# One hybrid encoder layer on one core: row factors put into the raw operands of the input projection

## The chip, the core and the metric

The kernel runs on one core of a Trainium2 chip. The core has a matrix engine (TensorE, PE in the profile, with PEld for its weight loads), a vector engine (VectorE, DVE), a scalar engine (ScalarE, ACT), a general engine (GpSimd, POOL), a queue engine (SyncE, SP) that issues most of the transfers, and transfer engines (DMA). Each engine works off its own queue in order; semaphores tie the queues together. Operands lie in on-chip memory, matmul sums in PSUM. The metric is the device time of one execution in microseconds, lower is better.

## The reference

One layer of a streaming encoder: token mixing, cross-attention into 256 memory tokens, and a SwiGLU feed-forward part, each between two RMS norms, for 2048 tokens of 1024 numbers in float32. What matters here is the start:

```python
def rms_norm(x, g):
    xf = x.astype(jnp.float32)
    y = xf * lax.rsqrt(jnp.mean(xf * xf, axis=-1, keepdims=True) + RMS_EPS)
    return (y * g.astype(jnp.float32)).astype(x.dtype)
...
        u = rms_norm(h, g_mix_pre[l])
        z = u @ w_in[l]
        qa, ka, va, qh, fh, ih, gh = jnp.split(z, IN_SPLITS, axis=-1)
...
    qf = jax.nn.silu(q.astype(f32)) * (Dk ** -0.5)
...
    f = lbf + (1.0 - lbf) * jax.nn.sigmoid(f_logit.astype(f32))
...
    o = rms_norm(o, onorm_g) * jax.nn.silu(g.astype(f32))
```

The columns of z are split into queries, keys and values of a windowed attention (qa, ka, va) and four groups for a gated recurrence (qh through a silu, fh through a sigmoid, ih as it is, gh through a silu). A row's norm is a factor r of that token; the weight g belongs to the column of x.

## The kernel before

Every matrix product is done with float32 operands that are split into a rounded high part and a remainder (the low part); three matmuls (high x high, high x low, low x high) stand for one. For large products the kernel also saves matmuls by a seven-product scheme: two 2x2 block matrices are multiplied with seven block products in place of eight, at the cost of sums and differences of the operands and of the results.

The change concerns the first stage, `in_first` (from L440), which computes z for the first 1024 of the 2048 tokens, transposed (columns of w_in on the partitions). It goes through eleven blocks (`ORDER`, L427), each of two times 128 columns of z: block 0 is columns 4 and 5 (in units of 128), block 1 is 0 and 1, block 2 is 2 and 3, blocks 3 to 6 pair a column of fh (10 to 13) with one of qh (6 to 9), blocks 7 and 8 are ih (14 to 17), blocks 9 and 10 are gh (18 to 21). A block has a kind: "p", plain, with eight products in four steps (`eight`, L1132), or "o", with seven products in seven steps (`seven`, L1092, in the order 1, 5, 6, 3, 7, 2, 4). A product is 12 matmuls of 128x512. So a plain block is 96 matmuls and a seven-product block 84. Before the change, blocks 0 and 1 are plain.

The moving operand is x transposed, in four raw tiles `raw[q, s]` (q: half of the 1024 columns of x, s: half of the tokens). `first` (L457) multiplies a raw tile by the weight g and splits it, ACT for the high part, DVE for the low one; the four pairs are the operands named 1, 2, 8 and 3 of the products (tiles named u in the profile). `gained` (L466) puts g into the raw tiles themselves, with ACT. From these, `resident` (L959) makes the operands of the seven products that are sums or differences (5, 7, 6, 4 in this order; DVE at L981, in place), each in two halves of 128x1024, split by `split2` (L949: ACT at L952, DVE at L955; tiles named T). 1, 2 and 3 are taken over from `first`. `phases` (L1169) writes out the order: after each step it makes the weight operands of the step after next, advances the generators that stand beside the blocks (twice a step in a plain block), finishes one half of an operand (`split`) and starts another (`half`). Operands that are a raw block by themselves (1, 2, 3, 8) are finished two steps after they are started, and, by `behind` (L1015), behind whatever each engine already has; sums and differences have no such lag. Seven slots hold operands: four that hold the operands of `first` until their last use, and three more, of which two hold the staged rows of x at the start.

The weight operands of a block come through `streamed` (L1030): two raw tiles are loaded, seven operands are formed by DVE sums (L1057), split by ACT or POOL for the high part and by DVE (L955) for the low part; tiles named S.

The norm is applied to the products, not to x. `rows` loads the 1024 rows of x (L477), `squares` (L480) sums their squares on ACT, POOL makes r of it (L108 and L111 in `rstd`), `spread` (L490) turns r into a 128x512 tile by transposes on PE, and `known` (L498) has ACT copy it into `r_bc` (L501), beside block 2. Blocks whose outputs come before that (0 and 1) copy them out bare (L590) and are multiplied by r_bc on POOL later (L620). In the others `out` (L582) multiplies each 128x512 output: by DVE straight from PSUM where there is nothing to add (L593, one a block), else DVE adds a stored part (L595) and POOL multiplies (L596, three a block). Then fh goes through ACT's tanh (L598) and POOL (L600); qh and gh through tanh (L604) and DVE (L605). A block of fh and qh then runs the decays of the recurrence (`decays`, L688) in the time of the block behind it: logarithm on ACT (L693), two scans on DVE (L697), POOL subtracts (L702), exponentials on ACT (L711, L713), products on DVE (L716, L628).

The order on each engine is not quite the written one: a scheduler that is fed with the written order moves an instruction ahead where it expects its engine to be free.

Of the kernel before, what the change touches and what calls it, by code (L numbers as in the profile page):

```python
# [11 lines left out]
F32 = mybir.dt.float32  # L12
F32R = mybir.dt.float32r
I32 = mybir.dt.int32
AF = mybir.ActivationFunctionType
# [33 lines left out]
class Layer:  # L49
# [390 lines left out]
    def in_first(self):  # L440
# [6 lines left out]
        key = {(0, 0): 1, (1, 0): 2, (0, 1): 8, (1, 1): 3}  # L447
        self.r_bc = None

# [15 lines left out]

        def gained(q, s):  # L466
            for k in range(4):
                nc.scalar.activation(raw[q, s][:, k, :], raw[q, s][:, k, :], AF.Copy,
                                     scale=g_t[:, 4 * q + k:4 * q + k + 1])

        def rows():

            for s in range(2):
                stage.append(self.tb.tile([P, 4, D], F32, tag="T", name=f"x0_{s}", bufs=3))
            for s in range(2):
                for i in range(4):
                    self.load(stage[s][:, i, :], I["x"][(4 * s + i) * P:(4 * s + i + 1) * P, :])  # L477
# [20 lines left out]
        def known():  # L498
            r = self.gain_tile()
            for s in range(2):  # L500
                nc.scalar.activation(r[:, s * 512:(s + 1) * 512], spread(0, s), AF.Copy)  # L501
            self.r_bc = r
            yield

# [24 lines left out]
        def parted():  # L529
            for n in (1, 3, 2, 0):  # L530
# [5 lines left out]
                with self.behind() if n else contextlib.nullcontext():  # L536
# [29 lines left out]
    def in_block(self, ca, cb, beside, get, between):  # L566
# [15 lines left out]
        def out(i, j, a, b):  # L582
            if not z:
                z.append(self.pair_tile())
                bare.append(self.r_bc is None)
            c0 = (ca, cb)[i] * P
            sl = slice(j * 512, (j + 1) * 512)
            zs = z[0][:, i, sl]
            if bare[0]:
                nc.scalar.activation(zs, a, AF.Copy)  # L590
                return
            if b is None:
                nc.vector.tensor_tensor(zs, a, self.r_bc[:, sl], ALU.mult)  # L593
            else:
                nc.vector.tensor_tensor(zs, a, b, ALU.add)  # L595
                nc.gpsimd.tensor_tensor(zs, zs, self.r_bc[:, sl], ALU.mult)  # L596
# [572 lines left out]
    def phases(self, jobs, first, prologue=None):  # L1169
# [18 lines left out]
        for g, (n, i, p) in enumerate(steps):  # L1188
            key = (n, p, i > len(jobs[n][2]) // 2 if p == 8 else 0)
# [64 lines left out]
        class Ready(dict):  # L1254


            def __getitem__(_, p):
                q = next(q for q in range(g, len(steps)) if steps[q][2] == p)
                n, i, _ = steps[q]
                key = (n, p, i > len(jobs[n][2]) // 2 if p == 8 else 0)  # L1260
                while left.get(key, 1):
# [489 lines left out]
```

## Time and profile before

| what | value |
|---|---|
| time, median of 3 runs (lowest to highest) | 2576.51 us (2575.25 to 2578.38) |
| the profiled execution: its time; its span | 2576.22 us; 2574.5 us |
| mean granted TensorE clock | 0.994 |
| matmuls | 12000 |
| busy PE, DVE, ACT, POOL | 2515.8, 1766.2, 1258.9, 518.3 us |
| read from and written to HBM | 330.45 MB, 162.53 MB |

The stage of the change takes the first 256 us of the span; what follows it is not touched. In rows of the profile, `out<-in` are the program's tiles, x is a count, and after the bar stand the busy time of the group in us, the mean duration of one in ns, and the idle time of the engine ahead of them with what ended it. In a timeline, a row is the start and the duration in us, the engine, the line and the operation, and in brackets the engine's idle time before it. In a table of stretches, PEclk is the granted TensorE clock as a share of full speed.

### The profile page before, as it was taken

To read this page: it belongs to the slowest core of one execution; us is meant where nothing else is said; L and a number is where in the kernel's file an instruction comes from. 1 tells how busy PE (TensorE), PEld (TensorE's weight loads), DVE (VectorE), ACT (ScalarE), POOL (GpSimd) and SP (SyncE) were. 2 spreads that over 40 slices of the span, in tenths; PEclk is the share of its full clock that TensorE was granted. 3 is DMA by queue.
4 is the path that set the end of the run, shared out by engine and by line. 5 is a ranking of instruction groups with operands and counts; after the bars stand their busy time and mean duration, and the time that the engine had idled before them with its cause. 6 is when DMAs were issued, how large, how long until landed. Compare 5 with 4: busy or idle time off the path is not lost. (4 is left out here: it accounts for less than half of the span.)

```text
span 2574.5 us, 34140 instructions
## 1 busy us (share of the span) xinstructions
PE 2515.8 (98%) x12000; PEld 2093.7 (81%) x12000; DVE 1766.2 (69%) x2790; ACT 1258.9 (49%) x2632; POOL 518.3 (20%) x666
## 2 busy tenths in 40 slices
PE   8989999999999999999999999999999999999998
PEld 6767788878897888888788888888888888888886
DVE  7777678877766678697775665575666566664756
ACT  7452366655655575565564333353333344543443
POOL 2663343321321334224310000000000000000022
PEclk9999999999999999999999999999999999999999
DMA  5452655484896787767983552253555434566798
GB/s 198 138 203 95 199 151 173 132 258 160 262 315 236 229 279 212 244 230 209 313 264 126 167 165 81 82 196 123 181 195 197 159 129 140 194 217 191 222 223 206
DMA packets 277835, 495.22 MB, mean 192 GB/s; under 512 B 20896, under 2 KB 135584, under 8 KB 277152
## 3 DMA queue, kind: packets, MB, share of 16 engines
q1 hardware_dynamic: 264128, 443.76, 51.5%
q0 software_dynamic: 11232, 40.90, 8.4%
q10 hardware_dynamic: 2304, 8.39, 0.8%
q8 instruction: 94, 1.54, 0.2%
q14 instruction: 77, 0.63, 0.1%
HBM read 330.45 MB, written 162.53 MB: 191 GB/s over the span
## 5 line engine op out<-in xcount | busy, mean ns | idle before, releaser
L1088 PE MATMUL psm<-T,S 128*128 128x512 f32 x2664 | 1032.7, 391 | 8.6 <-ACT S L952 4.4
L1089 PE MATMUL psm<-T,S 128*128 128x512 f32 x2664 | 1039.3, 390 | 0.0
L1090 PE MATMUL psm<-T,S 128*128 128x512 f32 x2664 | 1033.1, 390 | 1.5 <-DVE S L955 1.5
L1088 PEld LDWEIGHTS psm<-T,S 128*128 128x128 f32 x2664 | 501.0, 188 | 116.0 <-ACT S L952 5.2
L1090 PEld LDWEIGHTS psm<-T,S 128*128 128x128 f32 x2664 | 500.8, 188 | 107.3 <-DVE S L955 3.1
L1089 PEld LDWEIGHTS psm<-T,S 128*128 128x128 f32 x2664 | 501.2, 188 | 102.9
L952 ACT ACTIVATE S<-sum 128x512 fp32r<-128x512 f32 (+1 forms) x338 | 207.2, 617 | 331.7 <-PE psm L1090 328.9
L955 DVE TENSOR_TENSOR S<-sraw,S 128x512 fp32r<-128x512 f32 (+1 forms) x311 | 217.1, 704 | 212.8 <-ACT S L952 203.2
L955 DVE TENSOR_TENSOR S<-sum,S 128x512 fp32r<-128x512 f32 (+1 forms) x404 | 283.7, 707 | 81.8 <-ACT S L952 67.3
L1103 ACT ACTIVATE part<-psm 128x512 f32<-128x512 f32 x297 | 174.7, 591 | 204.1 <-PE psm L1090 197.0
L952 ACT ACTIVATE S<-sraw 128x512 fp32r<-128x512 f32 (+1 forms) x272 | 166.4, 617 | 154.8 <-PE psm L1090 149.5
L1458 POOL DMA_DIRECT2D row<-y_d x28 | 25.1, 895 | 1071.2 <-DMA sraw<-hid_d 905.3
L1429 ACT ACTIVATE junk<-row 128x512 f32<-128x512 f32 x160 | 99.6, 624 | 95.2 <-DVE row L1451 32.8
L172 PE MATMUL psg<-u,wlo 128*128 128x512 f32 x352 | 141.6, 402 | 2.4 <-DVE wlo L153 2.4
L955 DVE TENSOR_TENSOR T<-row,T 128x1024 fp32r<-128x1024 f32 x104 | 124.1, 1202 | 27.7 <-ACT T L952 27.3
L170 PE MATMUL psg<-u,whi 128*128 128x512 f32 x352 | 142.7, 406 | 0.0
L171 PE MATMUL psg<-u,whi 128*128 128x512 f32 x352 | 141.8, 403 | 0.0
L952 ACT ACTIVATE T<-row 128x1024 fp32r<-128x1024 f32 x104 | 105.3, 1023 | 20.5 <-DMA row<-in_w_down_dram 9.9
L1633 DVE TENSOR_TENSOR part<-psm,part 128x512 f32<-128x512 f32 x66 | 45.5, 689 | 65.7 <-PE psm L1090 65.6
L954 POOL TENSOR_SCALAR S<-sum 128x512 fp32r<-128x512 f32 x66 | 50.3, 763 | 183.5 <-PE psm L1090 105.5
L1090 PE MATMUL psm<-u,S 128*128 128x512 f32 x172 | 71.4, 418 | 13.1 <-DVE S L955 13.1
L1624 DVE TENSOR_TENSOR row<-psm,part 128x512 f32<-128x512 f32 x66 | 45.5, 689 | 54.7 <-PE psm L1090 54.6
(326 smaller groups left out, 3664.2 us busy)
## 6 DMA issues: line engine op xcount, KB each, us to landing
sraw<-in_w_gate_dram SPq DMA_DIRECT2D x44, 512.0 KB, 4.8
sraw<-in_w_up_dram SPq DMA_DIRECT2D x44, 512.0 KB, 5.0
hid_d<-row SPq DMA_DIRECT2D x44, 512.0 KB, 2.7
h_d<-row SPq DMA_DIRECT2D x32, 512.0 KB, 6.6
y_d<-row SPq DMA_DIRECT2D x32, 512.0 KB, 3.6
sraw<-hid_d SPq DMA_DIRECT2D x32, 512.0 KB, 5.0
row<-h_d POOLq DMA_DIRECT2D x30, 512.0 KB, 7.1
row<-y_d POOLq DMA_DIRECT2D x28, 512.0 KB, 7.6
```

The costliest lines, as they stand in the source:

```text
L170: nc.tensor.matmul(ps, ah, bh, start=(i == 0), stop=False)
L171: nc.tensor.matmul(ps, ah, bl, start=False, stop=False)
L172: nc.tensor.matmul(ps, al, bh, start=False, stop=(i == n - 1))
L952: self.nc.scalar.activation(hi, raw, AF.Copy)
L954: self.nc.gpsimd.tensor_scalar(hi, raw, 1.0, 1.0, ALU.mult, ALU.mult)
L955: self.nc.vector.tensor_tensor(lo, raw, f32(hi), ALU.subtract)
L1088: nc.tensor.matmul(ps, s[:, 0, k, :], t[:, 0, k, :], start=st, stop=False, **kw)
L1089: nc.tensor.matmul(ps, s[:, 0, k, :], t[:, 1, k, :], start=False, stop=False, **kw)
L1090: nc.tensor.matmul(ps, s[:, 1, k, :], t[:, 0, k, :], start=False, stop=sp, **kw)
L1103: nc.scalar.activation(t, ps, AF.Copy)
L1429: self.nc.scalar.activation(junk, a, AF.Square, scale=float(D) ** -0.5, accum_out=to)
L1624: nc.vector.tensor_tensor(d, a, c, ALU.add)
```

## The change

Three blocks are plain instead of two. They work on operands from x times g, without r, as blocks 0 and 1 did. Once r is known for half of the tokens, DVE multiplies the raw tiles in place by g and r (r read from PSUM). All seven operands of the seven-product blocks (3 to 10) are then made from these normed raw tiles, so their outputs need no factor. `gained` is gone; the first four tiles of rows of x are loaded right behind the transposed x, and the other four within block 0; the squares move from block 1 to block 0 and `known` from block 2 to block 1. The seven products become a second job of `phases`, and no operand of it is started until `held` is cleared at the end of `known`. Operand 3 is put ahead of 7, since 7 is formed in place on the raw tile of 3. Outputs of blocks 1 and 2 are multiplied by r on DVE from PSUM; block 0's are multiplied on POOL later, as before. In blocks 3 to 10 an output of ih that has nothing to be added to is copied by ACT, and the tanh and the product behind it read PSUM where nothing is added.

```diff
+        self.r_bc = self.r_half = None
+        self.held = True
...
-        def gained(q, s):
-            for k in range(4):
-                nc.scalar.activation(raw[q, s][:, k, :], raw[q, s][:, k, :], AF.Copy,
-                                     scale=g_t[:, 4 * q + k:4 * q + k + 1])
...
+        def rows(s):
+            stage.append(self.tb.tile([P, 4, D], F32, tag="T", name=f"x0_{s}", bufs=3))
+            for i in range(4):
+                self.load(stage[s][:, i, :], I["x"][(4 * s + i) * P:(4 * s + i + 1) * P, :])
 
         def squares():
 
+            rows(1)
             for s in range(2):
...
         def known():
             r = self.gain_tile()
             for s in range(2):
-                nc.scalar.activation(r[:, s * 512:(s + 1) * 512], spread(0, s), AF.Copy)
-            self.r_bc = r
-            yield
+                ps = spread(0, s)
+                nc.scalar.activation(r[:, s * 512:(s + 1) * 512], ps, AF.Copy)
+                self.r_bc = r if s else self.r_bc
+                self.r_half = r
+                for q in ((0, 1), (1, 0))[s]:
+                    for k in range(4):
+                        t = raw[q, s][:, k, :]
+                        nc.vector.scalar_tensor_tensor(t, t, g_t[:, 4 * q + k:4 * q + k + 1], ps, ALU.mult, ALU.mult)
+                    yield
+                if s == 0:
+                    yield
+            self.held = False
...
-        beside = [(), (), (0, 1), (2, 3), (4, 5), (6,), (7,), (), (), (), ()]
+        beside = [(), (), (), (0, 1), (2, 3), (4, 5), (6, 7), (), (), (), ()]
         get = fetch()
-        blocks = [("p" if i < 2 else "o",)
+        blocks = [("p" if i < 3 else "o",)
...
-        job = (lambda i, j, a, n: raw[i, j][:, a:a + n, :], 4, blocks, None,
-               {0: [rows], 1: [squares], 2: [known], 8: [scaled], 10: [parted]})
-        phases = self.phases([job], T)
+        jobs = [(of, 4, blocks[:3], None, {0: [squares], 1: [known]}),
+                (of, 4, blocks[3:], None, {5: [scaled], 7: [parted]})]
+        phases = self.phases(jobs, T)
...
+        rows(0)
         first(0, 0)
...
-        for q, s in ((1, 1), (0, 1), (0, 0), (1, 0)):
-            gained(q, s)
         self.mix_consts()
...
             if b is None:
-                nc.vector.tensor_tensor(zs, a, self.r_bc[:, sl], ALU.mult)
+                if ca < 6:
+                    nc.vector.tensor_tensor(zs, a, self.r_half[:, sl], ALU.mult)
+                    return
             else:
                 nc.vector.tensor_tensor(zs, a, b, ALU.add)
-                nc.gpsimd.tensor_tensor(zs, zs, self.r_bc[:, sl], ALU.mult)
-            if C_FH <= c0 < C_IH:
-                nc.scalar.activation(zs, zs, AF.Tanh, scale=0.5)
+                a = zs
+            if C_IH <= c0 < C_GH:
+                if b is None:
+                    nc.scalar.activation(zs, a, AF.Copy)
+            elif C_FH <= c0 < C_IH:
+                nc.scalar.activation(zs, a, AF.Tanh, scale=0.5)
                 h = (c0 - C_FH) // P
                 nc.gpsimd.tensor_scalar(zs, zs, self.fb[:, h:h + 1], self.fa[:, h:h + 1], ALU.mult, ALU.add)
-            elif C_QH <= c0 and not C_IH <= c0 < C_GH:
+            else:
...
-                nc.scalar.activation(t, zs, AF.Tanh, scale=0.5)
-                nc.vector.scalar_tensor_tensor(zs, t, 1.0, zs, ALU.add, ALU.mult)
+                nc.scalar.activation(t, a, AF.Tanh, scale=0.5)
+                nc.vector.scalar_tensor_tensor(zs, t, 1.0, a, ALU.add, ALU.mult)
...
-        queue = sorted(uses, key=lambda k: (uses[k][0] - (5 if k[1] == 7 and jobs[k[0]][3] is None else 0), k))
+        queue = sorted(uses, key=lambda k: (uses[k][0] - (5 if k[1] == 7 and jobs[k[0]][3] is None else
+                                                          6 if k[1] == 3 and first else 0), k))
...
-                if not queue:
+                if not queue or first and self.held:
                     return False
```

More of the change, by code (lines that the diff above doesn't have):

```diff
@@ L464, in first @@
                                                ALU.mult, ALU.subtract)
-        def gained(q, s):
-            for k in range(4):
-                nc.scalar.activation(raw[q, s][:, k, :], raw[q, s][:, k, :], AF.Copy,
-                                     scale=g_t[:, 4 * q + k:4 * q + k + 1])
[L471 to L477, printed above, removed]
-            yield
+        def rows(s):
+            stage.append(self.tb.tile([P, 4, D], F32, tag="T", name=f"x0_{s}", bufs=3))
+            for i in range(4):
+                self.load(stage[s][:, i, :], I["x"][(4 * s + i) * P:(4 * s + i + 1) * P, :])
         def squares():
+            rows(1)
             for s in range(2):
@@ L539, in parted, with of @@
                 u[s] += [(t[:, 0, k, :], t[:, 1, k, :]) for k in range(4)]
[L541 removed]
+        beside = [(), (), (), (0, 1), (2, 3), (4, 5), (6, 7), (), (), (), ()]
         get = fetch()
[L543 removed]
+        blocks = [("p" if i < 3 else "o",)
                   + self.in_block(*p, beside[i], get if i > 6 else (), None if i else lambda: x_load(0, 0))
                   for i, p in enumerate(self.ORDER)]
[L546 to L548 removed]
+        def of(i, j, a, n):
+            return raw[i, j][:, a:a + n, :]
+        jobs = [(of, 4, blocks[:3], None, {0: [squares], 1: [known]}),
+                (of, 4, blocks[3:], None, {5: [scaled], 7: [parted]})]
+        phases = self.phases(jobs, T)
         self.load(g_t, I["g_mix_t"])
@@ L1188, in phases @@
         for g, (n, i, p) in enumerate(steps):
-            key = (n, p, i > len(jobs[n][2]) // 2 if p == 8 else 0)
+            key = (n, p, i > len(jobs[n][2]) // 2 if p == 8 and not first else 0)
             uses.setdefault(key, []).append(g)
-        queue = sorted(uses, key=lambda k: (uses[k][0] - (5 if k[1] == 7 and jobs[k[0]][3] is None else 0), k))
+        queue = sorted(uses, key=lambda k: (uses[k][0] - (5 if k[1] == 7 and jobs[k[0]][3] is None else
+                                                          6 if k[1] == 3 and first else 0), k))
         slots = [("A", -2, i) for i in range(4)] + [("B", -1, i) for i in range(3)]
@@ L1259, in __getitem__ @@
                 n, i, _ = steps[q]
-                key = (n, p, i > len(jobs[n][2]) // 2 if p == 8 else 0)
+                key = (n, p, i > len(jobs[n][2]) // 2 if p == 8 and not first else 0)
                 while left.get(key, 1):
```

4 lines of the change are left out of this document (1 added, 3 removed).

## The prediction, made before the changed kernel was run

> **What bounds the kernel now.** I read the page first, then the busy times of each engine by stretch, then the waits of TensorE and the timelines around one wait.
>
> ```profile
> span 2574.5 us, 34140 instructions
> ...
> PE 2515.8 (98%) x12000; PEld 2093.7 (81%) x12000; DVE 1766.2 (69%) x2790; ACT 1258.9 (49%) x2632; POOL 518.3 (20%) x666
> ```
>
> TensorE is busy for 98% of the span, so only two things can move the end: the number of matmuls, and the few places where PE stands still or runs slowly. The change touches the first 256 us alone. There the stretches, cut at the blocks of the first half (block 2, 3, 4, 5, 6, 7, then 8 and 9, then 10), read:
>
> ```profile
> core 0: us, PE busy (x) PEld busy (x) DVE busy (x) ACT busy (x) POOL busy (x), PEclk, DMA share, GB/s
> 56.00:78.00 22.00, 22.00 (x101) 18.03 (x100) 11.91 (x13) 6.10 (x11) 15.90 (x10) 1.00 0.39 145
> 78.00:101.00 23.00, 23.00 (x101) 18.49 (x99) 18.73 (x22) 9.15 (x14) 12.76 (x12) 1.00 0.43 136
> 101.00:127.00 26.00, 21.79 (x85) 16.61 (x84) 19.91 (x21) 14.29 (x22) 16.48 (x17) 0.93 0.29 102
> 127.00:152.00 25.00, 20.87 (x83) 16.51 (x83) 18.84 (x22) 14.63 (x23) 15.43 (x17) 0.93 0.58 210
> 152.00:177.00 25.00, 21.81 (x87) 16.89 (x86) 20.03 (x24) 14.32 (x22) 16.02 (x18) 0.93 0.59 206
> 177.00:204.00 27.00, 24.51 (x102) 19.48 (x101) 20.28 (x28) 9.98 (x18) 13.29 (x15) 0.94 0.33 121
> 204.00:241.00 37.00, 36.98 (x163) 29.68 (x161) 30.81 (x41) 8.91 (x15) 13.91 (x13) 1.00 0.20 71
> 241.00:256.00 15.00, 14.12 (x59) 10.97 (x60) 9.01 (x13) 5.64 (x9) 7.68 (x6) 1.00 0.44 154
> ```
>
> Blocks 2 and 3 lose nothing. Blocks 4 to 7 lose 4.2 + 4.1 + 3.2 + 2.5 = 14.0 us of PE idle time, and their granted clock is 0.93 to 0.94: 0.07 of 26, 25 and 25 us and 0.06 of 27 us make another 6.9 us. In all 20.9 us can be won there, and hardly anything elsewhere. What the waits are, and how one of them comes about:
>
> ```profile
> L1090 PE MATMUL psm<-u,S 128*128 128x512 f32 x40 | 18.8, 471 | 13.1 <-DVE S L955 13.1
> ```
>
> ```profile
> 98.92 0.39 PE L1088 MATMUL psm<-T,S 128*128 128x512 f32 x1
> ...
> 100.79 0.40 PE L1090 MATMUL psm<-T,S 128*128 128x512 f32 x1
> ...
> 105.82 0.79 PE L1090 MATMUL psm<-u,S 128*128 128x512 f32 x1 [3.88 <-DVE S L955]
> 106.41 0.63 PE L1088 MATMUL psm<-u,S 128*128 128x512 f32 x1
> 106.84 0.63 PE L1089 MATMUL psm<-u,S 128*128 128x512 f32 x1
> ```
>
> ```profile
> 93.17 3.00 POOL L596 TENSOR_TENSOR pair<-pair,g 128x512 f32<-128x512 f32 x2 [0.63 <-DVE pair L595]
> ...
> 103.32 1.90 POOL L702 TENSOR_TENSOR pair<-pair,d_mid 128x1024 f32<-128x1024 f32 x1
> ```
>
> ```profile
> 93.61 3.11 DVE L955 TENSOR_TENSOR S<-sum,S 128x512 fp32r<-128x512 f32 x2
> ...
> 100.61 2.33 DVE L697 TENSOR_TENSOR_SCAN pair<-reset,pair 128x512 f32<-128x512 f32 x2
> 102.86 0.67 DVE L593 TENSOR_TENSOR pair<-psm,g 128x512 f32<-128x512 f32 x1
> 103.44 2.33 DVE L955 TENSOR_TENSOR S<-sraw,S 128x512 fp32r<-128x512 f32 x1
> ```
>
> The first two rows are eight matmuls apart, so matmuls start 0.234 us apart. At 105.82 one has waited 3.88 us for the low part of the block's first weight operand, a DVE subtraction (L955). That subtraction stood behind two scans of the decays and a multiplication by the row factors (L593), and then took 2.33 us because POOL's L702 ran beside it. The scans came late because POOL multiplied two outputs by the factors first (L596, 3.00 us) before ACT's tanh and POOL's L600 could go on. After the wait the next matmuls are 0.43 us apart for 1.5 us or so. All four waits (13.1 us) have this form. So the bound in blocks 4 to 7 is DVE's queue, stretched and fed late by POOL.
>
> **The change part by part.** Prices come from these rows of the first 260 us:
>
> ```profile
> L468 ACT ACTIVATE pair<-pair,g_t 128x512 f32<-128x512 f32 x16 | 11.2, 709 | 0.0
> ```
>
> ```profile
> L596 POOL TENSOR_TENSOR pair<-pair,g 128x512 f32<-128x512 f32 x27 | 42.3, 1574 | 25.3 <-DVE pair L595 25.0
> L620 POOL TENSOR_TENSOR pair<-pair,g 128x1024 f32<-128x1024 f32 x4 | 9.9, 2512 | 4.1 <-ACT g L501 4.1
> ```
>
> ```profile
> L955 DVE TENSOR_TENSOR S<-sum,S 128x512 fp32r<-128x512 f32 x36 | 34.9, 985 | 6.1 <-ACT S L952 3.4 <-POOL S L954 2.6
> L595 DVE TENSOR_TENSOR pair<-psm,part 128x512 f32<-128x512 f32 x27 | 18.3, 687 | 19.8 <-PE psm L1090 19.5 <-ACT part L1103 0.2
> L525 DVE SCALAR_TENSOR_TENSOR pair<-pair,g_t,pss 128x512 f32<-128x512 f32 x16 | 11.3, 740 | 0.0
> L955 DVE TENSOR_TENSOR T<-pair,T 128x1024 fp32r<-128x1024 f32 x8 | 10.0, 1269 | 0.7 <-ACT T L952 0.7
> L981 DVE TENSOR_TENSOR pair<-pair,pair 128x1024 f32<-128x1024 f32 x8 | 9.7, 1221 | 2.1 <-ACT pair L468 2.0
> L593 DVE TENSOR_TENSOR pair<-psm,g 128x512 f32<-128x512 f32 x9 | 6.1, 682 | 3.8 <-PE psm L1090 3.8
> ```
>
> *More matmuls.* Block 2 becomes plain: 8 products of 12 matmuls instead of 7, so 12 more, at 0.234 us: +2.8 us, on the path.
>
> *Scaling the raw operands.* Sixteen DVE instructions of the form of L525 (a tile, a column and PSUM, 740 ns): 11.8 us of DVE, instead of 16 ACT instructions (L468). Bounds by the nearest rows are 682 ns (L593) and 985 ns (L955 with both operands in tiles); I take 740, the same form. They need the row factors and are emitted behind the first and second step of block 1, which begins near 56 - 22.5 = 33.5 us (96 matmuls at 0.234 us are 22.5 us), so they run from about 39 us on. Today DVE makes the combined operands (L981, and L955 into T) in that block, and these now come later, so PE's work on block 1 covers the scaling and the cost is nothing. Without it, all 11.8 us would stand ahead of the operands of block 3.
>
> *All seven operands anew, and later.* Today the seven products of block 2 take three operands that block 0 already used, and only four are made (8 halves). Now all seven are made (14 halves), and none before the scaling is emitted, at the third step of block 1; the first half is moreover held behind the first step of block 2, which begins near 56 us. So from 56 us until the seventh product of block 3 starts (block 2 lasts 22.5 us, six products 16.8 us; together 39.3 us) DVE has: 14 subtractions and 8 combinations of 1.22 us each, 26.8; five outputs of plain blocks, 3.4; two splits for block 2, 1.4; seven splits and four sums for block 3, 7.6; two of block 3's additions, 1.4. That is 40.6 us at the undisturbed 0.69 us of L595, and about 2 more because POOL's two remaining L620 (2.5 us each) run beside it: 42.6 us against 39.3. I put the cost at the missing 3.3 us and a partial loss of clock, +4.0 us. Its lower bound is 0 (order and slack happen to fit). Its upper bound is three separate waits like the one at 105.82, each 3.3 us idle and 1.7 us of slow clock, +15 us. The second half of operand 1 is queued on DVE behind the last output of block 2, which waits for the last matmul of that block; whoever needs operands 5 and 6 waits behind it.
>
> *No factors on the outputs.* All 27 L596, two of the four L620, and the L593 of blocks 3 to 10 go; blocks 1 and 2 get eight such DVE outputs instead. What L596 costs DVE shows in the block above: two L955 took 3.11 us instead of 1.38 beside two L596, a stretch of 1.7 us. The 36 L955 of this kind are at 985 instead of 690 ns on the mean, whatever POOL instruction ran beside them, so not each block has so much; I take 1.5 us a block, and with the L593 (0.7) DVE is relieved by 2.2 us. Then 14.0 - 4 x 2.2 = 5.2 us of idle time is left in blocks 4 to 7, and I leave 2.6 us of slow clock (one or two of the four). Gain: 20.9 - 7.8 = -13.1 us. I do not count that tanh now starts without POOL, because that moves the scans but also moves L702 against other DVE work. Bounds: -2.8 us (only the L593 counts, 0.7 us a block, the clock still drops) and -20.9 us.
>
> The rule of the Trainium skill that bears on this is in "SBUF — State Buffer", Who interferes with whom: a DVE instruction with two inputs in SBUF and a GpSimd instruction that reads SBUF block each other for a whole instruction, one with a single such input does not. The trace agrees: L955 ended at 105.77, just after L702, while L593, L595 and L525, which read PSUM, stay at 0.68 to 0.74 us. By it the sixteen scalings are safe from POOL, which leaves the sum as it is.
>
> ```profile
> PE psg L172 <- DVE wlo L153: 2.4, 2, 1.5
> PE psm L1088 <- DVE pair L595: 0.9, 1, 0.9
> ```
>
> *The end of the stage.* These two waits of PE (250 to 270 us) come where POOL still multiplies outputs before it can round the next weights. I count half: -1.5 us, bounds 0 and -3.3.
>
> ```profile
> 43.32 1.88 POOL L111 TENSOR_TENSOR r_u<-n_v,mhalf 128x4 f32<-128x4 f32 x1
> ```
>
> ```profile
> 59.76 1.08 ACT L501 ACTIVATE g<-pss 128x512 f32<-128x512 f32 x2
> ```
>
> *Loads and factors.* The first four tiles of rows of x are loaded ahead of block 1's weights, the other four behind them. Today the second set of factors is ready at 45.2 us (L111) and used only at 59.76 (L501). In the new order ACT has no L468 ahead of the squares, so I expect the factors by 45 us as well, at or before the step that uses them, and count nothing; later than about 50 us they would cost what they are late.
>
> The sum: the profiled execution took 2576.22 us (1.7 us around its span; 0.3 below the median of the runs). 2576.2 + 2.8 + 4.0 - 13.1 - 1.5 = 2568.4 us.
>
> The Trainium skill, "TensorE: Matmul & The Clock Gate", HAM oscillation, gives idle gaps over some 3.4 us as what drops the clock. Here the trace differs: gaps below that dropped it too (13.1 us over four waits, the longest 3.9, and all four stretches at 0.93 to 0.94). By the page only the two longest would have a clock loss to win back, and the sum would be some 3 us higher.
>
> **The rivals.**
> 1. All waits go. For it: no L596 (1.57 us each) stands between an output and its tanh any more, so the scans leave the block's start. Against it: DVE's 18.84 us of block 5 less 2.2 are still 16.6 in a block of 84 x 0.234 = 19.7 us. 2576.2 + 2.8 + 1.0 - 20.9 - 3.3 = 2555.8 us.
> 2. L702, not L596, sets the waits. For it: it ran exactly beside the late L955. Against it: L596 delays the chain that L702 is part of. Gain 2.8 only: 2576.2 + 2.8 + 4.0 - 2.8 - 1.5 = 2578.7 us, no change.
> 3. The operands of block 3 arrive late, on the other side. DVE is over-full from 56 to 95 us, the waits come in three products (+15), and the backlog enters block 4 and halves the gain there (-6.5): 2576.2 + 2.8 + 15 - 6.5 - 1.5 = 2586.0 us. It decides from the point where the supply costs over 10 us while the gain is halved, or 17 us at the full gain. For it: 42.6 us of work for 39.3. Against it: the deadline falls one product at a time, and 56 to 78 us is DVE's emptiest stretch (11.91 of 22).
> 4. The factors come late, so the scaling is put off and every operand after it. For it: the second rows now load behind block 1's weights. Against it: ACT no longer does sixteen L468 before the squares. Ten us late eats the slack and costs about 10: 2578 us.
>
> **How the numbers follow.** Forecast 0.44, with its own range 2561 to 2572; rival 1 0.10; rival 2 0.15; rival 3 0.28; rival 4 0.03. About 0.2%, or 5 us, is what a measurement can tell from no change. Faster: 0.44 + 0.10 = 0.54; same: 0.15 + 0.03 = 0.18; slower: 0.28. The range 2557 to 2586 reaches to rivals 1 and 3 and leaves out the far half of the one and a part of the other.
>
> **What would show it.** Right: no POOL multiplications of 128x512 by the factors; granted clock 1.00 in at least two of blocks 4 to 7 and PE waits for L955 there of 5 us or less; DVE nearly full from 56 to 95 us with one or two short PE waits on T or S near block 3. Wrong: PE waits for T of 3 us and more, a clock below 1.00 in block 2 or 3, or four waits on S as long as now.

## The result, and the profile after

| what | before | after |
|---|---|---|
| time, median of 13 runs each, same sessions (lowest to highest) | 2579.94 us (2574.55 to 2586.51) | 2572.07 us (2567.57 to 2577.04) |
| ratio after to before, 95% interval | | 0.9972 [0.9962, 0.9982] |
| the profiled execution: its time; its span | 2576.22 us; 2574.5 us | 2571.13 us; 2569.4 us |

The changed kernel is faster: by the ratio 0.28%, or 7.2 us of 2580 (4.6 to 9.8 by the interval; the two medians are 7.9 us apart). The forecast was 7.8 us less than the profiled execution of before, 0.9970. The median of these thirteen runs of the kernel before lies 3.4 us above that of the three shown first, which are among them, so the ratio is what compares, not the two absolute times.

From the page of after, engine busy times; lines lie about ten further down than in the kernel before:

```profile
span 2569.4 us, 34131 instructions
...
PE 2517.3 (98%) x12012; PEld 2095.3 (82%) x12012; DVE 1751.8 (68%) x2801; ACT 1254.1 (49%) x2614; POOL 459.4 (18%) x637
```

Twelve matmuls came and POOL lost 59 us. The stretches of after, with the same cuts as in the prediction:

```profile
core 0: us, PE busy (x) PEld busy (x) DVE busy (x) ACT busy (x) POOL busy (x), PEclk, DMA share, GB/s
56.00:78.00 22.00, 22.00 (x95) 17.70 (x94) 20.38 (x24) 9.11 (x10) 1.71 (x1) 1.00 0.26 88
78.00:101.00 23.00, 22.31 (x97) 17.88 (x96) 20.15 (x26) 10.13 (x14) 3.94 (x4) 1.00 0.41 137
101.00:127.00 26.00, 22.32 (x95) 17.46 (x94) 20.71 (x24) 16.88 (x23) 13.61 (x14) 0.99 0.24 83
127.00:152.00 25.00, 23.63 (x95) 18.21 (x93) 20.19 (x27) 16.53 (x25) 12.89 (x19) 0.95 0.57 210
152.00:177.00 25.00, 21.64 (x85) 16.95 (x86) 18.47 (x24) 15.59 (x26) 11.27 (x15) 0.93 0.56 210
177.00:204.00 27.00, 27.00 (x113) 21.89 (x114) 16.34 (x25) 9.40 (x18) 6.30 (x10) 0.94 0.58 185
204.00:241.00 37.00, 36.52 (x161) 29.29 (x159) 25.97 (x41) 12.48 (x22) 5.67 (x10) 1.00 0.20 79
241.00:256.00 15.00, 12.23 (x51) 9.13 (x50) 9.76 (x12) 7.57 (x10) 3.37 (x5) 1.00 0.37 132
```

From 56 to 101 us DVE is nearly full (40.5 of 45 us, 30.6 before), and PE loses only 0.69 us there. From 101 to 204 us PE is idle for 3.7 + 1.4 + 3.4 + 0 = 8.4 us instead of 14.0, and the granted clock takes 0.26 + 1.25 + 1.75 + 1.62 = 4.9 us instead of 6.9: three of the four slow stretches are still there. What PE waited for, 20 to 270 us (total, times, longest):

```profile
PE psm L1100 <- DVE S L965: 5.0, 4, 1.9
PE psm L1098 <- DVE pair L602: 3.2, 2, 2.8
PE psg L170 <- POOL whi L152: 1.8, 1, 1.8
PE psm L1098 <- ACT part L1113: 1.2, 2, 0.7
```

The waits for the low part of a weight operand fell from 13.1 to 5.0 us. Other waits took their places: for an output's addition on DVE (L602, 3.2 us), and, at the end of the stage, for the first weights of the next one (1.8 us, L152).

The sum by the two traces. More matmuls +2.8; operands +0.7; blocks 4 to 7 from 20.9 to 13.3, -7.6; the end of the stage and the first 15 us behind it +1.6 (3.25 us idle and a slow stretch of 1.7, where before had 0.9 + 1.45 + 0.96 = 3.3 us idle); the start of the kernel -0.1 (the first matmul comes 0.5 us earlier, but more of the first ones are slow, and the 101st starts at 34.05 instead of 34.19 us). That is -2.6. ACT's first copy of values in the next stage, which I use as a landmark below, moved by 3.9, from 295.27 to 291.34 us (duration in ns; first and last start):

```profile
L750 ACT ACTIVATE vst<-pss x2: 215/216/218, 295.3 to 309.2; 128x64 fp32r<-128x64 f32 x2
```

```profile
L760 ACT ACTIVATE vst<-pss x2: 217/218/218, 291.3 to 306.6; 128x64 fp32r<-128x64 f32 x2
```

The other 1.3 us are order: the kernel before runs eight short matmuls of the next stage (L848, from 264.29 us, 0.16 us each) ahead of the landmark, and after runs them behind it, from 292.05 us. They are moved, not saved. Behind the landmark, in code that the change leaves alone, after gains another 1.2 us in spite of them, so the two profiled spans differ by 5.1 us, which lies in the interval. Where that gain arises no run shows.

### The profile page after: what moved, and what is told of

Read it like the earlier page. It is cut to its first block, busy times and chain, and to the rows that moved or that the text cites. A ratio compares the mean times of both kernels' runs of the same rounds, so it can differ in the third digit from the quotient of the medians.

```text
span 2569.4 us, 34131 instructions
## 1 busy us (share of the span) xinstructions
PE 2517.3 (98%) x12012; PEld 2095.3 (82%) x12012; DVE 1751.8 (68%) x2801; ACT 1254.1 (49%) x2614; POOL 459.4 (18%) x637
## 4 chain that ended last, share of the span: by engine, by line
PE 81%; DMA 7%; DVE 5%; issue 3%; POOL 2%; ACT 2%; SPq 0%; DVEq 0%; POOLq 0%; ACTq 0%
PE psm L1098 23%; PE psm L1100 22%; PE psm L1099 22%; PE psg L170 2%; PE psg L172 2%; PE psg L171 2%; PE pss L1351 1%; DVE S L965 1%; DMA qd<-z_d 1%; DMA row<-h_d 1%; DMA row<-d_s 1%; DMA kk<-z_d 1%; DMA row<-in_x_dram 1%; DVE T L965 1%; PE pss L811 0%
## 5 line engine op out<-in xcount | busy, mean ns | idle before, releaser
L1098 PE MATMUL psm<-T,S 128*128 128x512 f32 x2744 | 1063.1, 392 | 11.1 <-ACT S L962 4.5
L1100 PE MATMUL psm<-T,S 128*128 128x512 f32 x2744 | 1065.6, 391 | 8.0 <-DVE S L965 7.8
L1099 PE MATMUL psm<-T,S 128*128 128x512 f32 x2744 | 1071.6, 391 | 0.0
L1098 PEld LDWEIGHTS psm<-T,S 128*128 128x128 f32 x2744 | 516.4, 188 | 123.1 <-ACT S L962 6.5
L1100 PEld LDWEIGHTS psm<-T,S 128*128 128x128 f32 x2744 | 516.3, 188 | 120.0 <-DVE S L965 12.2
L1099 PEld LDWEIGHTS psm<-T,S 128*128 128x128 f32 x2744 | 516.4, 188 | 106.4
L965 DVE TENSOR_TENSOR S<-sraw,S 128x512 fp32r<-128x512 f32 (+1 forms) x312 | 213.0, 690 | 214.5 <-ACT S L962 200.1
L965 DVE TENSOR_TENSOR S<-sum,S 128x512 fp32r<-128x512 f32 (+1 forms) x400 | 275.9, 694 | 77.7 <-ACT S L962 59.8
L1113 ACT ACTIVATE part<-psm 128x512 f32<-128x512 f32 x294 | 172.9, 591 | 182.6 <-PE psm L1100 177.3
L965 DVE TENSOR_TENSOR T<-row,T 128x1024 fp32r<-128x1024 f32 x104 | 124.2, 1201 | 30.4 <-ACT T L962 30.2
L153 DVE TENSOR_TENSOR wlo<-raw,whi 128x1024 fp32r<-128x1024 f32 x54 | 69.3, 1283 | 23.1 <-ACT whi L150 18.4
L1635 DVE TENSOR_TENSOR row<-psm,part 128x512 f32<-128x512 f32 x66 | 45.4, 688 | 55.2 <-PE psm L1100 55.1
```

The source lines that it names most:

```text
L153: nc.vector.tensor_tensor(lo, raw, f32(hi), ALU.subtract)
L965: self.nc.vector.tensor_tensor(lo, raw, f32(hi), ALU.subtract)
L1098: nc.tensor.matmul(ps, s[:, 0, k, :], t[:, 0, k, :], start=st, stop=False, **kw)
L1099: nc.tensor.matmul(ps, s[:, 0, k, :], t[:, 1, k, :], start=False, stop=False, **kw)
L1100: nc.tensor.matmul(ps, s[:, 1, k, :], t[:, 0, k, :], start=False, stop=sp, **kw)
L1113: nc.scalar.activation(t, ps, AF.Copy)
```

## The experiments

Each kernel is one edit on the kernel before or after. "Landmark" is the start of the copy shown above. The start of the kernel moves it from one execution to the next: the 101st matmul, ahead of which no edit below changes PE's work, starts between 32.7 and 34.7 us, and what an edit moved is better read from the difference of the two columns. In before, third_plain, before_no_pool_factor and after_log_and_order the landmark also has the eight matmuls of L848 ahead of it (1.3 us). Ratios are to the kernel before, timed on the same chip.

| run | edit | 101st matmul, us | landmark, us | ratio [95% interval] |
|---|---|---|---|---|
| before | | 34.2 | 295.3 | 1 |
| after_again | the changed kernel, timed again | 33.9 | 291.3 | 0.9973 [0.9961, 0.9984] |
| third_plain | before, third block plain | 33.2 | 300.7 | 1.0005 [0.9994, 1.0017] |
| before_no_pool_factor | before, without L596 | 33.0 | 289.4 | 0.9976 [0.9965, 0.9988] |
| after_pool_in_chain | after, a multiplication on POOL as L596 | 33.8 | 302.5 | 1.0011 [1.0000, 1.0023] |
| after_pool_beside | after, the same on data nobody needs | 33.4 | 303.2 | 1.0004 [0.9992, 1.0015] |
| after_pool_memset | after, fills on POOL in its place | 34.7 | 288.3 | 0.9955 [0.9939, 0.9972] |
| after_mid_dve | after, subtraction of the decays on DVE | 32.7 | 292.3 | 0.9989 [0.9979, 0.9998] |
| after_three_S | after, weight tiles begin three further on | 32.9 | 289.9 | 0.9972 [0.9959, 0.9985] |
| after_both | the last two together | 34.4 | 295.4 | 0.9986 [0.9975, 0.9997] |
| after_one_before_seven | after, operand 1 made before 7 | 34.2 | 291.2 | 0.9964 [0.9952, 0.9976] |
| after_log_and_order | the last, and a shorter way to the logarithm | 34.0 | 293.6 | 0.9979 [0.9970, 0.9988] |
| after_split_twice | after, four more subtractions on DVE | 33.9 | 298.5 | 0.9989 [0.9980, 0.9999] |

### Where the gain comes from

The change does two things at once: a third plain block, which gives DVE more time, and outputs without factors. The first alone, on the kernel before:

```diff
-        blocks = [("p" if i < 2 else "o",)
+        blocks = [("p" if i < 3 else "o",)
```

> The kernel before, with block 2 made plain and nothing else changed. Theory A (the gain of the change comes from taking the row factors off the outputs, and the third plain block only costs its matmuls): the stage ends 12 x 0.234 = 2.8 us later, so the first matmul of the next stage starts near 259.1 us instead of 256.3; the four waits on S stay at 12 to 14 us. Rival B (the plain block itself helps, since it needs fewer weight operands from DVE and POOL): the stage ends at 256 us or earlier and the waits on S fall below 9 us.

Waits of PE in this kernel, 20 to 270 us:

```profile
PE psm L1090 <- DVE S L955: 9.7, 4, 3.9
PE psm L1088 <- ACT part L1103: 4.3, 2, 2.5
PE psm L1088 <- DVE pair L595: 3.6, 3, 1.4
```

No gain: the landmark is 5.4 us later, 2.8 of it the twelve matmuls. The waits on S fell by 3.4 us, but those on L1103 and L595 rose from 1.5 to 7.9 us. So more plain blocks relieve nothing by themselves; nor did the waits stay as they were.

The second alone, also on the kernel before, where 27 outputs then stay without their factor:

```diff
                 nc.vector.tensor_tensor(zs, a, b, ALU.add)
-                nc.gpsimd.tensor_tensor(zs, zs, self.r_bc[:, sl], ALU.mult)
```

> The kernel before without POOL's 27 multiplications of outputs by the row factors; those outputs stay without their factor. Theory A: the waits of PE on S (13.1 us before) fall to 5 us or less and the next stage starts 8 us or more earlier than 256.3 us. Rival C (POOL's subtraction in the decays sets these waits): they stay at 10 us or more and the next stage starts at 254 us or later.

```profile
PE psm L1089 <- DVE S L954: 8.6, 4, 2.7
```

The waits on S fell from 13.1 to 8.6 us, all four slow stretches stayed, and the landmark came 5.9 us earlier, 4.6 when the earlier start is taken off. That is less than the one theory expected and more than the other: POOL's multiplications are a large part of the waits, not the whole of them. The ratio, 0.9976, cannot be told from that of the whole change (0.9973): what the change does besides taking L596 away gives in sum nothing more that these runs can measure.

Then the same work put back into the changed kernel, as a multiplication by ones, first where L596 stood (between the addition and the tanh), then on the stored part, whose content nobody reads any more:

```diff
+        self.ones = self.mc.tile([P, 512], F32, name="ones")
+        nc.gpsimd.memset(self.ones, 1.0)
...
                 nc.vector.tensor_tensor(zs, a, b, ALU.add)
+                nc.gpsimd.tensor_tensor(zs, zs, self.ones, ALU.mult)
```

> The changed kernel, with POOL multiplying 24 outputs of blocks 3 to 10 (three a block) by a tile of ones between DVE's addition and the tanh, where the kernel before multiplied by the factors. Theory A: PE's waits on S and on outputs come back to 10 us or more and the next stage starts near 262 us (changed kernel: 254.5). Rival C: the next stage starts within 3 us of 254.5.

```diff
                 nc.vector.tensor_tensor(zs, a, b, ALU.add)
+                nc.gpsimd.tensor_tensor(b, b, self.ones, ALU.mult)
```

> The changed kernel, with the same 24 multiplications by ones on POOL, but of the stored part after DVE has added it: POOL is as busy beside DVE, and no tanh waits for it. If the multiplications cost by stretching DVE's instructions (theory A as predicted, 1.5 us a block): the next stage starts 5 us or more later than 254.5. If they cost by standing in the chain from an output to its scan: it starts within 2 us of 254.5.

Both lose the whole gain (landmarks 11.2 and 11.9 us later, ratios 1.0011 and 1.0004). The second is as dear as the first though no tanh waits for its results, so the delay of the chain behind the output is not needed to explain the cost. Two causes are left: POOL's queue is held, or DVE is disturbed while POOL reads. Fills hold the queue as long and read nothing:

```diff
                 nc.vector.tensor_tensor(zs, a, b, ALU.add)
+                for _ in range(3):
+                    nc.gpsimd.memset(b, 1.0)
```

> The changed kernel, with three POOL fills of 128x512 (about 0.52 us each, 1.55 us together) at each of the 24 places where the two runs before had one multiplication: POOL's queue is held as long, but the fills read no tile. If POOL's multiplications cost by stretching DVE's instructions beside them: DVE's split and sum groups stay at the changed kernel's means (961, 859 and about 700 ns between 100 and 200 us) and the next stage starts within 2.5 us of 254.5. If they cost by holding POOL's own queue (splits, decays): it starts 6 us or more later, as with the multiplications (263.3, 263.7).

The groups of 78 to 205 us that matter, for the kernel before, after, after_pool_beside and after_pool_memset in turn (count, busy us, mean ns of one, then the idle time ahead):

```profile
L955 DVE TENSOR_TENSOR S<-sum,S 128x512 fp32r<-128x512 f32 x22 | 20.3, 932 | 5.6 <-ACT S L952 3.4 <-POOL S L954 2.1
L955 DVE TENSOR_TENSOR S<-sraw,S 128x512 fp32r<-128x512 f32 x17 | 16.7, 983 | 1.2 <-ACT S L952 1.2
```

```profile
L965 DVE TENSOR_TENSOR S<-sum,S 128x512 fp32r<-128x512 f32 x23 | 20.9, 912 | 4.4 <-POOL S L964 4.4
L965 DVE TENSOR_TENSOR S<-sraw,S 128x512 fp32r<-128x512 f32 x18 | 15.1, 842 | 3.2 <-ACT S L962 2.7 <-POOL S L964 0.5
```

```profile
L605 POOL TENSOR_TENSOR part<-part,ones 128x512 f32<-128x512 f32 x15 | 25.7, 1711 | 21.3 <-DVE pair L604 21.3
L968 DVE TENSOR_TENSOR S<-sum,S 128x512 fp32r<-128x512 f32 x21 | 21.6, 1037 | 4.8 <-POOL S L967 4.6 <-ACT S L965 0.2
L968 DVE TENSOR_TENSOR S<-sraw,S 128x512 fp32r<-128x512 f32 x15 | 14.2, 953 | 0.5 <-POOL S L967 0.5
```

```profile
L604 POOL MEMSET part<- 128x512 f32 x48 | 25.2, 526 | 13.1 <-DVE pair L602 12.0
L967 DVE TENSOR_TENSOR S<-sum,S 128x512 fp32r<-128x512 f32 x23 | 19.2, 843 | 3.2 <-POOL S L966 3.2
L967 DVE TENSOR_TENSOR S<-sraw,S 128x512 fp32r<-128x512 f32 x18 | 15.2, 846 | 2.3 <-ACT S L964 1.4 <-POOL S L966 0.9
```

POOL is held for 25.7 and 25.2 us at the same places. Beside the multiplications DVE's subtractions take 1037 and 953 ns, beside the fills 843 and 846, in after 912 and 842. Taken over all subtractions and sums of these stretches, the time above 690 ns each adds up to 16.9 us in before, 8.1 in after, 14.3 with the multiplications and 6.7 with the fills; in before_no_pool_factor it is 8.1. The landmark of the fills is 3 us earlier than that of after, that of the multiplications 12 us later. So it is the multiplication beside DVE that costs, not the hold on POOL's queue. The fills differ from it in two things: they read nothing, and they come in pieces of 526 instead of 1711 ns; no run parts the two. The rule of the Trainium skill in "SBUF — State Buffer", Who interferes with whom, makes just the first distinction: a DVE instruction with two inputs in SBUF contends with a GpSimd instruction that reads it, not with one that only writes. These runs agree (1037 against 843 ns).

In after_pool_in_chain the same sum is only 10.3 us, 2.2 above after where after_pool_beside has 6.2, and yet it lost as much at the landmark. There DVE's scans are stretched more (1413 ns on the mean, against 1257 in after_pool_beside and 1213 in after), and the tanh waits for POOL; no run parts what each of them costs.

The fills are the fastest kernel of the study by its median of four runs (2569.66 us), but its interval overlaps that of after; why it was fast stands in the last section.

### What is left in blocks 4 to 7

POOL still reads in the decays (L712). That one moved to DVE:

```diff
-        nc.gpsimd.tensor_tensor(b16, b16, mid.unsqueeze(2).broadcast_to([P, NCB, 64]), ALU.subtract)
+        nc.vector.tensor_tensor(b16, b16, mid.unsqueeze(2).broadcast_to([P, NCB, 64]), ALU.subtract)
```

> The changed kernel with the decays' 128x1024 subtraction on DVE instead of POOL. Theory F (the waits on S that are left come from this POOL instruction, which stretches the DVE split that runs beside it by about 1.6 us): PE's waits on S fall from 5.0 to 2 us or less, two or three slow-clock stretches go, and the next stage starts 4 to 7 us earlier than 254.5. Rival G (DVE is simply full there): DVE has 1.2 us more a block, the waits stay or grow, and the next stage starts at 254.5 or later.

```profile
L965 DVE TENSOR_TENSOR S<-sum,S 128x512 fp32r<-128x512 f32 x22 | 15.2, 700 | 7.3 <-POOL S L964 7.3
L965 DVE TENSOR_TENSOR S<-sraw,S 128x512 fp32r<-128x512 f32 x18 | 12.6, 707 | 4.6 <-ACT S L962 2.6 <-POOL S L964 2.1
```

```profile
153.11 0.50 PE L1100 MATMUL psm<-T,S 128*128 128x512 f32 x1 [1.88 <-DVE S L965]
177.87 0.62 PE L1100 MATMUL psm<-T,S 128*128 128x512 f32 x1 [1.89 <-DVE S L965]
```

The stretch is gone (700 and 707 ns), and yet two waits of 1.9 us stand where after has them (153.13 and 176.82 us), and others were added; the kernel was 4.4 us slower than after_again in the same session (2576.64 against 2572.20 us). This does not show that the stretch in after is harmless: in its place the edit gives DVE 5.4 us more work. In after the DVE rows ahead of the wait that ends at 153.13 us hold about 2.5 us of stretch (L965 2.35 us, L615 and L965 1.09 us each), in after_mid_dve DVE's own L712 (1.46 us) and the product L726 (1.62 us), which there runs ahead of the split of the block's first weight operand. Whether stretch or order sets the waits of blocks 6 and 7 stays open; no run moved that split alone. The largest wait of after, in block 5, comes about in another way, first PE's row, then DVE's:

```profile
125.64 0.50 PE L1098 MATMUL psm<-T,S 128*128 128x512 f32 x1 [2.77 <-DVE pair L602]
```

```profile
122.66 2.34 DVE L707 TENSOR_TENSOR_SCAN pair<-reset,pair 128x512 f32<-128x512 f32 x2 [2.03 <-ACT pair L703]
124.91 0.67 DVE L602 TENSOR_TENSOR pair<-psm,part 128x512 f32<-128x512 f32 x1
```

DVE stands still for 2.03 us ahead of two scans, because ACT's logarithm (L703) is not there, and the addition that PE needs is queued behind the scans. after_log_and_order lets ACT take the logarithm straight from the tanh (the affine step as its scale and bias, POOL's affine step behind it), together with the order of the next section:

```diff
-                h = (c0 - C_FH) // P
-                nc.gpsimd.tensor_scalar(zs, zs, self.fb[:, h:h + 1], self.fa[:, h:h + 1], ALU.mult, ALU.add)
...
-        nc.scalar.activation(e1, f, AF.Ln)
+            nc.scalar.activation(e1, f, AF.Ln, bias=fa, scale=fb)
+            nc.gpsimd.tensor_scalar(f, f, fb, fa, ALU.mult, ALU.add)
```

> The same order, and ACT takes the logarithm of the decays straight from the tanh, with the affine step as its scale and bias, while POOL's affine step runs once for 1024 columns behind it. If the waits left in blocks 4 to 7 come from the chain from tanh to scan: scans start about 1.2 us or more earlier, the waits on S and on outputs (5.0 and 3.2 us) fall by half or more, and 2 to 5 us more are gained than by the order alone. If they come from the order on DVE and ACT at the start of a block, less than 1 us.

It brought nothing: the scans of block 5 start at 120.85 us, still behind a wait of 2.05 us for the logarithm, and PE's wait on L602 there is 2.97 us. ACT's rows in after, ahead of the logarithm, show why:

```profile
119.63 0.61 ACT L608 ACTIVATE pair<-pair 128x512 f32<-128x512 f32 x1
120.27 1.28 ACT L703 ACT_TABLE_LOAD   x1
```

Between the tanh and the logarithm ACT loads a table for 1.28 us. POOL's step (L610, 0.91 us from 120.36 us) ran beside that load, so taking it away won nothing: in after_log_and_order the load still stands there (118.28 to 119.56 us), and from the end of the tanh to the start of the logarithm it is 1.32 us in both kernels.

### What the operands of block 3 cost

DVE gets 4 x 1.22 = 4.9 us more work in the crowded part, by making the low parts of operands 1 and 3 twice:

```diff
+            if key in (1, 3) and not sums:
+                nc.vector.tensor_tensor(dst[:, 1, a:b], t, f32(dst[:, 0, a:b]), ALU.subtract)
```

> The changed kernel with DVE making the low parts of operands 1 and 3 twice (four more subtractions of 1.22 us, 4.9 us, in blocks 1 to 3). If DVE has no slack there, as the prediction had it: PE waits 4 us or more longer before 101 us than the 0.7 us of the changed kernel. If PE's order gives way (products of block 4 run before the late ones of block 3): less than 2 us longer.

Waits of PE from 56 to 101 us in this kernel; after has 0.7 us there, on L1113 alone:

```profile
PE psm L1101 <- DVE T L965: 2.2, 1, 2.2
PE psm L1100 <- POOL S L964: 0.8, 1, 0.8
PE psm L1100 <- ACT part L1115: 0.7, 1, 0.7
```

3.0 us of the 4.9 came through as waiting, and a slow stretch behind it. So DVE had about 2 us to spare where the prediction had it 3.3 us short; the result lies between the two expectations.

### The end of the stage

Before, the first weights of the next stage are loaded from 240.98 us on; in after they come later. SP's queue in after (start, duration, three transfers):

```profile
248.75 1.28 SPq L75 DMA_DIRECT2D raw<-in_w_in_dram  x3
```

POOL's and PE's rows behind it:

```profile
252.63 1.79 POOL L152 TENSOR_SCALAR whi<-raw 128x1024 fp32r<-128x1024 f32 x1 [13.70 <-PE psm L1100]
```

```profile
254.47 0.50 PE L170 MATMUL psg<-u,whi 128*128 128x512 f32 x1 [1.84 <-POOL whi L152]
```

The room for these weights was held by something. Either by weight tiles (S) or by the slot of an operand that has its last use late. The first was tried by beginning the rotation of the S tiles three further on:

```diff
+        for i in range(3):
+            nc.gpsimd.memset(self.ts.tile([P, 2, 4, P], F32, tag="S", name=f"S_empty{i}", bufs=5)[:, 0, 0, 0:8], 0.0)
```

> The changed kernel with three weight-operand tiles taken and given back at the very start, so that as many such tiles are taken in all as before the change (71 and not 68) and the last ones lie in the same buffers as before. Theory D (the wait at the end of the stage comes because the next stage's first weights are loaded into room that the last products' weight operands still hold): the load is issued near 241 us as before and not at 248.8, the wait on POOL's rounding (1.8 us) goes, and the stage after it is 2 to 4 us earlier. Rival E (POOL or DVE are late there for another reason): no change, within 0.5 us.

> The two edits together. If D and F hold, the gains add: 6 to 11 us below the changed kernel, a ratio to the kernel before of 0.993 to 0.995. If only one holds, the gain of that one alone.

The load stayed late (247.51 us) and the wait of 1.8 us stayed too, so it isn't the S tiles; with the subtraction on DVE as well (after_both) the landmark came 4.1 us later than in after. The second: the order in which the operands are made decides whose slot comes free last.

```diff
-        queue = sorted(uses, key=lambda k: (uses[k][0] - (5 if k[1] == 7 and jobs[k[0]][3] is None else
+        queue = sorted(uses, key=lambda k: (uses[k][0] - ((4 if first else 5) if k[1] == 7 and jobs[k[0]][3] is None else
```

> The changed kernel with operand 1 made before operand 7, so that the room into which the next stage's first weights are loaded was operand 1's and not operand 7's, whose last use is later. Theory D2 (the wait at the end of the stage is this load): it is issued 7 us or more before the end of the stage's matmuls instead of 3.5 us, the 1.8 us wait on the rounded weights goes, and perhaps the slow clock behind it: 2 to 4 us better at the 61st matmul of the next stage (changed kernel: 271.0). Rival E: no change, within 0.5 us.

```profile
232.05 13.21 SPq L75 DMA_DIRECT2D raw<-in_w_in_dram  x3
```

```profile
PE psg L172 <- DVE wlo L153: 2.1, 1, 2.1
```

The load starts at 232.05 us and POOL's part is ready in time: the slot of operand 7 it was. But PE now waits 2.1 us for the low part (L153) of the same weights, behind splits on DVE, and the slow stretch remains. The landmark moved by 0.1 us. One wait had covered the other.

## Why the prediction was right, point by point

**What bounds the kernel.** Right: the gain came from blocks 4 to 7 and from DVE's queue there. That POOL's multiplications cost by stretching DVE was shown by after_pool_beside against after_pool_memset. That L596 also delays the chain of the decays was a part of the prediction's story; no run isolates it. after_pool_beside shows that a cost arises without it, and after_pool_in_chain, with less stretch and the same loss, that it may have had a share.

**More matmuls, +2.8.** As forecast: 12012.

**Scaling the raw operands, nothing.** Right, and with the price of the row that it was taken from:

```profile
40.00 5.35 DVE L501 SCALAR_TENSOR_TENSOR pair<-pair,g_t,pss 128x512 f32<-128x512 f32 x8 [2.88 <-ACT g L495]
```

Sixteen took 10.7 us (740 ns for one, partly overlapping), between 40 and 52 us, beside a PE that never waited. So the factors were not late either, and rival 4 did not come.

**Operands of block 3, +4.0.** Mis-sized: 0.7 us. DVE was nearly full, as forecast. But the deadline was taken too hard:

```profile
101.34 1.22 DVE L965 TENSOR_TENSOR T<-pair,T 128x1024 fp32r<-128x1024 f32 x1
```

The last half of the last operand is ready only at 102.6 us, 7 us behind the time that I gave it (95.3), and PE waits nowhere between 85.4 and 113.8 us: the scheduler put products of the next block ahead of it. The sum also counted DVE work from 56 us on, though the first halves were in work at 48.8 us on ACT and 55.2 us on DVE. after_split_twice puts the slack at 2 us, so rival 3 was near: five more microseconds of DVE work cost 7.2 us at the landmark.

**Factors off the outputs, -13.1.** The step that was mis-sized most: -7.6. Its first half held: waits on S of 5.0 us were measured where 5.2 us of idle time were forecast, and the stretch fell by 16.9 - 8.1 = 8.8 us from 78 to 205 us, five blocks, 1.8 us a block where the prediction took 1.5. Two things were left out. Relieving one wait uncovered another of 3.2 us on L602. And the clock: I had one or two slow stretches left of four, and three stayed, at waits of 2.77, 1.92 and 1.93 us where before had 3.80, 2.93 and 2.49. Shorter waits still cost the full 1.7 us each. So one sign that the prediction named for itself did not come: the clock stayed at 1.00 in block 4 alone (the first slow stretch begins at 126.31 us), not in two blocks. Its reading that the matmuls behind a wait are slow for 1.5 us or so was short, too: in before they run slow from 105.82 to 108.95 us, 3.1 us, of which about half is lost.

**End of the stage, -1.5.** Wrong in sign, +1.6: the multiplications are gone from POOL, and the load took the place of the delay because its room was held by operand 7.

**Rivals.** Rival 1 (all waits go) fell with the 8.4 us that are left. Rival 2 (L702 sets the waits, no change) fell: without L596 alone the landmark came 5.9 us earlier (4.6 without the start). after_mid_dve, where L702's stretch is gone, won nothing, but there DVE has its work instead, so it says little on this.

**The total.** It came out closer than its terms. The four terms sum to 2.8 + 0.7 - 7.6 + 1.6 = -2.5 in the traces, where the forecast had -7.8: too dear by 3.3 at the operands, too hopeful by 5.5 in blocks 4 to 7 and by 3.1 at the end of the stage. The start of the kernel (0.1), the eight matmuls that moved behind the landmark (1.3) and the 1.2 behind it bring the profiled pair to -5.1, and the runs as a whole gave -7.2. So the sign and the mechanism are shown, but the terms of the sum account for about a third of the measured gain, and that the size agrees within 1 us is mostly luck. The wide range, 2557 to 2586 us, also held no change and a slower kernel, so that the time lies in it says little.

## What to carry to other kernels

Price an engine's work also by what it does to its neighbour's instructions: 24 multiplications that nobody waited for cost 12 us beside DVE, and fills of the same length cost nothing. When a queue is relieved, ask which wait stood just behind the one that goes (here L602, and L153 behind L152): in both places the next wait took a part or all of the gain. When a step is taken out of a chain, ask what ran beside it (here a table load of ACT). And a wait of PE that is cut from 2.9 to 1.9 us has not yet won back the clock.

## What the runs showed of the hardware that I had not expected

The clock falls in steps of 3.41 us, on a fixed grid, and what counts is the idle time within one step. In after the slow rows begin just behind a wait of 1.93 us:

```profile
176.82 0.50 PE L1100 MATMUL psm<-T,S 128*128 128x512 f32 x1 [1.93 <-DVE S L965]
...
177.72 0.63 PE L1100 MATMUL psm<-T,S 128*128 128x512 f32 x1
178.15 0.63 PE L1098 MATMUL psm<-T,S 128*128 128x512 f32 x1
```

The slow rows of the block before begin at 153.75 us and those of block 5 at 126.52: 24.0 and 51.2 us earlier, 7 and 15 times 3.41. In after_split_twice a longer wait leaves the clock at full speed, since matmuls stay 0.234 us apart, and a shorter one does not:

```profile
130.51 0.50 PE L1100 MATMUL psm<-T,S 128*128 128x512 f32 x1 [2.75 <-DVE pair L602]
130.84 0.40 PE L1101 MATMUL psm<-T,S 128*128 128x512 f32 x1
131.08 0.40 PE L1102 MATMUL psm<-T,S 128*128 128x512 f32 x1
```

```profile
159.83 0.72 PE L1102 MATMUL psm<-T,S 128*128 128x512 f32 x1 [1.92 <-DVE S L965]
160.34 0.63 PE L1100 MATMUL psm<-T,S 128*128 128x512 f32 x1
```

The granted clock fell to 0.50 at 159.93 us; nine steps of 3.413 us earlier a boundary lies at 129.21 us. The wait that ended at 130.51 began at 127.76 and is cut by it into 1.45 and 1.30 us. In after_pool_memset waits of 1.64 and 1.27 us in blocks 6 and 7 left the clock alone where after loses it at 1.92 and 1.93: two slow stretches less, 3.4 us, nearly the whole lead of that kernel at the landmark (3.1 us, 3.7 when its later start is taken off). How far that is the edit and how far luck of the order no run separates. The slow steps, at a granted clock of 0.50, fix the grid in each of the fourteen traces. From 52 to 272 us a step at full clock with up to 1.85 us of idle PE in it (the most is from 158.33 us on in after_pool_beside) was never followed by a slow one, and a step with 1.87 us or more always was, 51 times. Behind 272 us the border is less sharp: 1.61 us was enough in after_mid_dve (from 789.1 us), and 1.89 us was not in after_again (from 778.3 us). So the exact point stays open. "TensorE: Matmul & The Clock Gate" of the Trainium skill describes such a free-running window of 3413 ns (section What's actually happening), and these spacings agree; that it takes a gap over some 3.4 us (HAM oscillation) does not hold here, where gaps of 1.92 and 1.93 us were enough.
